# Where the weights and the moving operands of TensorE's products lie in the state buffer, modulo 256 bytes

## The chip, the core and the metric

The kernel runs on one core of a Trainium2 chip. The metric is the device time of one execution in microseconds (us). Before the change it is 2124.55 us, the median of three runs (2123.25 to 2124.76).

## The reference

One decoder layer for 512 tokens of width 2048, in float32:

```python
mod = silu(c) @ w_ada + b_ada                    # 6 x 2048: shifts, scales, gates
h   = rms_norm(x, g1) * (1 + sc1) + sh1
u   = h @ w_in                                   # split into conv and attention groups
y   = [rms_norm(short_conv(u)) | rms_norm(nsa_attention(u))]
x   = x + gate1 * (y @ w_out)
h   = rms_norm(x, g2) * (1 + sc2) + sh2
x   = x + gate2 * (relu(h @ w_ff1)**2 @ w_ff2)   # hidden width 8192
out = rms_norm(x, gf)
```

The attention has 8 heads in 2 groups with three branches (compressed keys, selected blocks, a window). What matters here are the large products: the projections from `h`, the two halves of the output projection, and the two feed-forward products.

## The kernel before

**Every large product is three.** A float32 operand is kept as a high part (rounded to the type float32r) and a low part (the rest). The function `mm3` issues high weights by high tokens, high weights by low tokens, and low weights by high tokens. The stationary operand of a TensorE instruction (the weights, 128 x 128 numbers, 512 bytes in each partition) is loaded by its own instruction ahead of the product; the moving operand has 512 columns (2048 bytes in each partition) or 256 (1024 bytes). ScalarE makes the high part and VectorE the low part of each weight tile after its DMA has landed (`weights` in the first stages, `hilo` in the last).

**Three stages**, each recorded into an `Order` and laid out by its planner. The planner gives each instruction a price (`price`; for TensorE 0.0015 us plus 0.000453 us a column), simulates engines, DMA and buffers in a list schedule, and emits the instructions in the order of the simulated beginnings. Products marked `floating` are placed wherever the plan has their inputs ready; others keep the order of their lanes.

1. *Projections and convolution* (to about 555 us): 512-column products. Weights come through `raw` (three tiles of the pool `stage`) into `wh` and `wl` (two each). The tokens are 16 tiles `h`: seven of them in the pool `side` (in the trace `h`), nine in main slots (`h_m`).
2. *Attention and the first half of the output projection* (to about 750 us): scores on `kslc` and `kwin`, transposes, `pv` products on `tt`, and 512-column products `pw` on `mix`, which lies in main slots.
3. *The rest*, from about 750 us. First the products on `mixa`: eight weight blobs with 512 columns (two still from `stage`, six through `hl_tile()`), then `late_out(0)` and `late_out(1)`, 256 columns each on eight kept blobs: three in `hl` tiles, one in `sg`, one in `gt`, three in main slots (`kw`). Each half ends in a norm (`half_norm`), whose few fp32 products with `ones` float into the stream of the others. Then the feed-forward.

**The feed-forward** uses a scheme of seven products for a 2 x 2 block product, with 256 columns each. `part` runs the first three blocks of hidden units (24 parts), `ff1(p)` the other 29; each `ff1(p)` makes seven weight operands and issues 7 x 24 products. Results go to DRAM by the GpSimd queue (`outcome`, from `gt` and `gb`), and come back as tokens `tk` for the second half, which for every f and q again makes seven operands with 4 + 4 times 12 products (7 x 24). `plain(3)` at the end does the last columns without the scheme.

**Addresses.** All tokens `tk`, `h_m`, `mix`, `mixa` lie in main slots of 4096 bytes, the first at byte 34304 of the partition, so all at multiples of 256. The tiles `h` lie 128 past a multiple of 256, `wh` and `wl` too; `tt` at 128, `vcmp` and `kslc` at 32, the feed-forward's `sg` and `gt` at 0. Within a tile the blocks of weights are 512 bytes and the blocks of tokens 1024 or 2048 bytes apart, so a whole tile has one difference. So the difference of the weights' address minus the moving operand's, modulo 256, is 128 for 512-column products on `h_m` and `mix`, and 0 for those on `h`.

The operands `wh, wl` of the feed-forward come from a ring of three `hl` tiles of 8640 bytes, in turn at bytes 203264, 220544 and 211904, and start at a shifting place in them:

```python
def hl_tile():
    j, t = next(hl)
    lo = (16 * shift[0] - j * HLW) % (16 * NSHIFT)
    return t[:, lo:lo + 1024], t[:, lo + 1024:lo + 2048]
```

`shift[0]` is p mod 8 in the first half and (4f + q) mod 8 in the second. With shift s the three turns of the ring start at 64s, 64s + 192 and 64s + 64 bytes modulo 256. So successive operands of one pass cycle through three of the four differences 0, 64, 128 and 192, and with s through all. One operand is 24 products in a row.

Of the kernel before, what the change touches and what calls it, by code (L numbers as in the profile page):

```python
# [9 lines left out]
F32 = mybir.dt.float32  # L10
F32R = mybir.dt.float32r
# [5 lines left out]
P = 128  # L17
# [11 lines left out]
BLOB = 1072  # L29
# [2 lines left out]
NSIDE = 7  # L32
NWA = 8
NBANK = 6
NSHIFT = 8
SLACK = 4.0
FAST = 395e3

# [2 lines left out]
C_COS, C_SIN, C_MASK, C_CMASK, C_ROW, C_END = 0, 512, 1024, 1152, 1280, 1281  # L41
# [3 lines left out]
class Order:  # L45
# [46 lines left out]
    def price(self, eng, op, out, ins, kw):  # L92

        n = Order.width(out)
        if "dma" in op:
            return (0.42 if eng == "sync" else 0.55), 0.0
        if eng == "tensor":
            if op == "matmul" and ins[0].dtype == F32:
                return max(0.25, n * 0.00182), 0.2
            return (0.109 if op == "transpose" else max(0.06, 0.0015 + n * 0.000453)), 0.2  # L100
        if eng == "scalar":
            aps = len(ins) - 1
            more = 0.1 if kw.get("accum_out") is not None else 0.0
            return (0.18 if n < 16 else 0.09 + 0.00084 * n + (0.09 * max(0, aps) if not more else 0.19)), 0.16
        if n < 16:
            return 0.1, 0.14
        if op == "scalar_tensor_tensor":
            return 0.14 + 0.00101 * n, 0.14
        if op in ("tensor_scalar", "tensor_copy", "memset"):
            return 0.13 + 0.0005 * n, 0.14  # L110
        if op == "tensor_reduce":
            n = max(Order.width(x) for x in ins) * (1.7 if n > 16 else 1)
        return 0.068 + 0.00104 * n, 0.14
# [177 lines left out]
def hybrid_layer(ctx: ExitStack, tc: tile.TileContext, a, out):  # L291
# [8 lines left out]
    attc = front.enter_context(tc.tile_pool(name="attc", bufs=1))  # L300
    stage = front.enter_context(tc.tile_pool(name="stage", bufs=2))
# [10 lines left out]
    ts = [small.tile([P, T], F32, name="t", tag="t", bufs=5) for _ in range(5)]  # L312
    scr, temps = ts[0].bitcast(BF16), cycle(ts[1:])
    accums = cycle([small.tile([P, T], F32, name="sacc", tag="acc2k", bufs=2) for _ in range(2)])
    wraw = cycle([stage.tile([P, BLOB], F32, name="raw", bufs=3) for _ in range(3)])
    whl = cycle([[stage.tile([P, BLOB + 16], F32R, name=n) for n in ("wh", "wl")] for _ in range(2)])
    accs = cycle([small.tile([P, 2], F32, name="acc") for _ in range(4)])

# [28 lines left out]
    def weights(src, cols=1024, spare=False):  # L347
        raw = next(wraw)[:, :cols]
        nc.sync.dma_start(out=raw, in_=src)
        wh, wl = (slot(F32R, name="sw") for _ in range(2)) if spare else next(whl)  # L350
        wh, wl = wh[:, :cols], wl[:, :cols]
        nc.scalar.activation(wh, raw, AF.Copy)
        nc.vector.tensor_tensor(out=wl, in0=raw, in1=wh.bitcast(F32), op=OP.subtract)
        return wh, wl
# [5 lines left out]
    def mm3(ps, lh, ll, rh, rl, start, stop, more=False):  # L360
        nc.tensor.matmul(ps, lh, rh, start=start, stop=False, skip_group_check=more)
        nc.tensor.matmul(ps, lh, rl, start=False, stop=False, skip_group_check=more)
        nc.tensor.matmul(ps, ll, rh, start=False, stop=stop, skip_group_check=more)
# [7 lines left out]
    ident = vec[:, V_ID:V_END]  # L371
    for i in range(NK // 2):
        nc.sync.dma_start(out=xs[i], in_=a["xt"][i])
    cst = attc.tile([P, C_END - C_MASK], F32, name="cst")
    cmask = cst[:, C_CMASK - C_MASK:C_ROW - C_MASK].rearrange("p (b n) -> p b n", b=NQ)
    rowv = cst[:, C_ROW - C_MASK:]
    mask = cst[:, :C_CMASK - C_MASK]
# [244 lines left out]
    for s, (name, k) in enumerate(steps[:-1]):  # L622
# [5 lines left out]
        wh, wl = w  # L628
# [96 lines left out]
    cw2 = pair(name="cw2").rearrange("p a b -> p (a b)")[:, :576]  # L725
    nc.sync.dma_start(out=cw2, in_=a["vec"][:, V_END:])

    edges = [[attc.tile([P, 66], F32R, name=f"edge{i}{j}") for j in range(2)] for i in range(2)]
    for e in edges:
        for x in e:  # L730
# [78 lines left out]
    for j in range(8):  # L809
# [4 lines left out]
        for i in range(3):  # L814
            n = 3 * j + i
# [30 lines left out]
    for g in range(NG):  # L846
        pv = [bank() for _ in range(NQ)]
        for blk in range(4):
            wh, wl = weights(a["w_v"][g * 4 + blk], BLOB)
            more_ada(1)  # L850
            for j in range(4):
                k = blk * 4 + j
# [45 lines left out]
    for g in range(NG):  # L898
        pq = [bank() for _ in range(NR)]
        ks = list(range(NK)) if g == 0 else list(range(8, NK)) + [6, 7] + list(range(6))  # L900
        for i, k in enumerate(ks):
            if i % 2 == 0:
                wh, wl = weights(a["w_q"][g * 8 + k // 2])
# [178 lines left out]
    while m < NK:  # L1082
        out_conv(m)
        m += 1
    oa = [weights(a["w_oa"][k]) for k in range(2)]
# [9 lines left out]
    ffp = ffn.enter_context(tc.tile_pool(name="ffp", bufs=2, reuse_waits="tile"))  # L1095
    psf = ffn.enter_context(tc.tile_pool(name="psf", bufs=8, space=PSUM, reuse_waits="tile"))
    HT = T // 2
    rw = cycle([ffp.tile([P, 1024], F32, name="rw", bufs=6) for _ in range(6)])
    gt = cycle([ffp.tile([P, 2, 2, HT], F32R, name="gt", bufs=3) for _ in range(3)])
    gb = cycle([ffp.tile([P, 2, HT], F32R, name="gb", bufs=1)])  # L1100
    p1s = cycle([ffp.tile([P, HT], F32, name="p1", bufs=3) for _ in range(3)])
    sg = {t: cycle([ffp.tile([P, 1024], d, name="sg", bufs=2) for _ in range(2)])
          for t, d in (("first", F32R), ("sums", F32), ("last", F32R))}
    HLW = 2048 + 16 * (NSHIFT - 1)
    hl = cycle([(j, ffp.tile([P, HLW], F32R, name="hl", bufs=3)) for j in range(3)])
    shift = [0]
    banks = cycle([psf.tile([P, T], F32, name="pf") for _ in range(8)])
    LO, HI = slice(0, HT), slice(HT, T)
    halves = (LO, HI)
# [2 lines left out]
    def bankf():  # L1112
        return next(banks)

    def raw_blob(src):
        raw = next(rw)
        nc.sync.dma_start(out=raw, in_=src)
        return raw

    def hl_tile():  # L1120
        j, t = next(hl)
        lo = (16 * shift[0] - j * HLW) % (16 * NSHIFT)
        return t[:, lo:lo + 1024], t[:, lo + 1024:lo + 2048]

    def hilo(dst, src, minus=False):
        if minus:
            nc.scalar.activation(dst[0], src, AF.Copy, scale=-1.0)
            nc.vector.scalar_tensor_tensor(out=dst[1], in0=src, scalar=-1.0, in1=dst[0].bitcast(F32),
                                           op0=OP.mult, op1=OP.subtract)
        else:  # L1130
            nc.scalar.activation(dst[0], src, AF.Copy)
            nc.vector.tensor_tensor(out=dst[1], in0=src, in1=dst[0].bitcast(F32), op=OP.subtract)
        return dst
# [18 lines left out]
    sacc = accum()  # L1152
    pm = [bankf() for _ in range(8)]
    for k in range(8):
        wh, wl = oa[k] if k < 2 else hilo(hl_tile(), raw_blob(a["w_oa"][k]))
        for i in range(8):
            s = slice(i * P, (i + 1) * P)
            mm3(pm[i], wh[:, s], wl[:, s], mixa[k][:, 0], mixa[k][:, 1], k == 0, k == 7)
# [41 lines left out]
    def tslot():  # L1200
        return slot(F32R, name="tk")[:, :4 * HT].rearrange("p (k h t) -> p k h t", k=2, h=2)
# [5 lines left out]
    def sub(dst, x, y, op=OP.subtract):  # L1207
        nc.vector.tensor_tensor(out=dst, in0=x, in1=y, op=op)
# [187 lines left out]
        if n in (17, 19, 23):  # L1396
            results_of({17: 2, 19: 0, 23: 1}[n])
    for p in range(NP, 32):
        shift[0] = p % NSHIFT
        ff1(p)  # L1400


# [84 lines left out]
    for f in range(8):  # L1487
        for i in range(7):
            for j in range(2):
                tok[i][j] = tslot()  # L1490
                nc.sync.dma_start(out=tok[i][j].bitcast(F32), in_=gd[f][i][j].bitcast(F32))
            if f == 0 and i == T5:
                residual_pairs()
        last = f == 7
        for q in range(3 if last else 4):
            shift[0] = (4 * f + q) % NSHIFT
            raw = [raw_blob(a["w_f2"][4 * f + q, b]) for b in range(4)]
            ps = [{}, {}]
            for i, w in enumerate(operands(raw)):
                if f == 0 and q < 3 and i == B2:  # L1500
                    residual_pairs()
                ch, first, end = CHAIN[i]
                for j in range(2):
                    mp = 2 * q + j
                    m = 2 * mp
                    if first:
                        ps[j][ch] = bankf()
                    run(ps[j][ch], w, tok[i], first, True, 4 * j, 4)
                    b = ps[j][ch][:, :HT]
                    if i == B1:  # L1510
                        if f == 0:
                            nc.scalar.activation(base[mp], b, AF.Copy)
                        else:
                            sub(base[mp], b, base[mp], OP.add)
                        if last:
                            shared(mp)
                    elif i == U6:
                        update(m, HI, b, True)
                    elif i == T5:
                        update(m + 1, HI, b, True)  # L1520
                    elif i == B2:
                        update(m, LO, b)
                        if last:
                            final(m, LO)
                    elif i == T7:
                        update(m + 1, HI, b)
                        if last:
                            final(m + 1, HI)
                    elif i == B3:
                        update(m, HI, b)  # L1530
                        if last:
                            final(m, HI)
                    else:
                        update(m + 1, LO, b)
                        if last:
                            final(m + 1, LO)
# [92 lines left out]
```

## Time and profile before

| | |
|---|---|
| median of 3 runs | 2124.55 us (2123.25 to 2124.76) |
| the profiled execution | 2124.95 us |
| its span, first to last instruction | 2123.2 us |
| TensorE products, weight loads | 14978, 14978 |
| mean granted TensorE clock | 0.994 of full speed |

Nearly all instructions pass through one helper, so the profile gives them one line (L121), and groups are told apart by their tiles: `pf<-tk,hl` is a product into a feed-forward bank with tokens `tk` and weights `hl`. The profile's mean time of one product (280 ns for 256 columns) is that from its start to its modelled end; products overlap, so the time that one costs in a stream is the distance from its start to the next one's start. A row of the timeline is a run of like instructions: start of the first, us to the end of the last, count. A row of the table by windows gives the busy time of each engine in a stretch, with the count of instructions that fall into it wholly or partly.

### The profile page before, as it was taken

How to read it: one execution, taken by the hardware profiler on the slowest of the kernel's cores; microseconds unless marked ns; L12 is line 12 of the kernel's file. 1: busy time of each engine (PE TensorE's matmuls, PEld its weight loads, DVE VectorE, ACT ScalarE, POOL GpSimd, SP SyncE). 2: the span in 40 equal slices, each digit the busy share in tenths (PEclk: the TensorE clock that was granted, in tenths of full speed). 3: DMA queues.
4: the chain of work that ended last, by engine and by line, in shares of the span. 5: the costliest groups of instructions: out<-in, count | busy, mean ns of one | idle time of the engine just before them, and what ended most of it. 6: DMA issues, size and time to landing. Idle time of an engine off the chain costs nothing.

```text
span 2123.2 us, 37933 instructions
## 1 busy us (share of the span) xinstructions
PE 2088.0 (98%) x14978; PEld 1941.9 (91%) x14978; DVE 1897.1 (89%) x3036; ACT 1006.0 (47%) x1472; POOL 128.2 (6%) x244
## 2 busy tenths in 40 slices
PE   7999999999999999999999999999999999999998
PEld 5888878898777789999999999999999999999997
DVE  8989988888998657999999999999998999999998
ACT  4432433222555435766666566666433333333345
POOL 0000000000000001021111211111000000000000
PEclk8999999999999999999999999999999999999999
DMA  8895689888421244476666666668876466366452
GB/s 341 338 351 217 219 295 323 303 290 290 148 80 40 70 168 159 145 220 217 194 199 204 204 199 198 214 193 302 307 265 218 139 248 236 126 244 236 134 188 90
DMA packets 143106, 454.17 MB, mean 214 GB/s; under 512 B 15824, under 2 KB 18128, under 8 KB 142928
## 3 DMA queue, kind: packets, MB, share of 16 engines
q1 hardware_dynamic: 108304, 386.72, 52.0%
q0 software_dynamic: 34048, 63.98, 9.6%
q8 instruction: 118, 1.93, 0.4%
q10 hardware_dynamic: 576, 1.05, 0.1%
q14 instruction: 60, 0.49, 0.1%
HBM read 383.53 MB, written 68.16 MB: 213 GB/s over the span
## 4 chain that ended last, share of the span: by engine, by line
PE 87%; DVE 9%; DMA 2%; issue 1%; ACT 1%; SPq 0%; DVEq 0%; ACTq 0%
PE pf L121 61%; PE ps L121 21%; PE pw L121 2%; DVE t L121 1%; PE pv L121 1%; DVE wl L121 1%; DVE nm L121 1%; DMA rw<-in_w_f 1%; DVE x L121 1%; DMA wa<-in_w_ada 1%; PE pt L121 1%; DVE tt L121 1%; DVE hl L121 1%; PE s L121 1%; DVE p L121 1%
## 5 line engine op out<-in xcount | busy, mean ns | idle before, releaser
L121 PE MATMUL pf<-tk,hl 128*128 128x256 f32 x10704 | 1251.4, 280 | 1.0 <-DVE x L121 0.5
L121 PEld LDWEIGHTS pf<-tk,hl 128*128 128x128 f32 x10704 | 1250.0, 189 | 1.4 <-issue 0.7
L121 ACT ACTIVATE hl<-rw 128x1024 fp32r<-128x1024 f32 x269 | 285.0, 1060 | 345.4 <-PE pf L121 291.2
L121 DVE TENSOR_TENSOR hl<-rw,hl 128x1024 fp32r<-128x1024 f32 x269 | 328.7, 1222 | 44.3 <-ACT hl L121 43.9
L121 ACT ACTIVATE hl<-sg 128x1024 fp32r<-128x1024 f32 x180 | 191.0, 1062 | 243.0 <-PE pf L121 222.1
L121 DVE SCALAR_TENSOR_TENSOR t<-wa,cs 128x1024 bf16<-128x1024 f32 x190 | 232.0, 1221 | 9.7 <-DMA wa<-in_w_ada 8.3
L121 PE MATMUL ps<-h_m,wh 128*128 128x512 f32 x720 | 227.7, 395 | 0.9 <-DVE h_m L121 0.9
L121 ACT ACTIVATE wh<-raw 128x1024 fp32r<-128x1024 f32 (+1 forms) x106 | 112.6, 1062 | 236.9 <-PE ps L121 200.8
L121 DVE TENSOR_TENSOR hl<-sg,hl 128x1024 fp32r<-128x1024 f32 x151 | 184.6, 1222 | 31.7 <-ACT hl L121 30.9
L121 PE MATMUL ps<-h,wh 128*128 128x512 f32 x560 | 172.7, 395 | 4.3 <-ACT h L121 4.3
L121 PEld LDWEIGHTS ps<-h_m,wh 128*128 128x128 f32 x720 | 134.9, 188 | 32.7 <-DVE h_m L121 1.2
L121 DVE TENSOR_TENSOR wl<-raw,wh 128x1024 fp32r<-128x1024 f32 (+1 forms) x106 | 129.9, 1226 | 30.1 <-ACT wh L121 29.7
L121 DVE SCALAR_TENSOR_TENSOR x<-pf,mod,x 128x256 f32<-128x256 f32 (+1 forms) x280 | 132.6, 488 | 17.1 <-PE pf L121 15.4
L121 DVE TENSOR_TENSOR sg<-sg,rw 128x1024 f32<-128x1024 f32 x120 | 146.2, 1219 | 0.0
L121 PE MATMUL ps<-h_m,wl 128*128 128x512 f32 x360 | 142.5, 396 | 0.0
L121 PEld LDWEIGHTS ps<-h,wh 128*128 128x128 f32 x560 | 105.6, 190 | 28.7 <-ACT h L121 6.7
L121 POOL DMA_DIRECT2D g<-gt x192 | 101.2, 532 | 373.1 <-issue 190.5
L121 PE MATMUL ps<-h,wl 128*128 128x512 f32 x280 | 106.2, 392 | 0.0
L121 PE MATMUL pw<-mix,wh 128*128 128x512 f32 x256 | 87.6, 404 | 0.0
L121 PEld LDWEIGHTS ps<-h_m,wl 128*128 128x128 f32 x360 | 67.7, 188 | 15.8
L121 DVE TENSOR_TENSOR sg<-rw 128x1024 f32<-128x1024 f32 x60 | 73.2, 1220 | 9.9 <-DMA rw<-in_w_f 6.8
L121 ACT ACTIVATE t<-t 128x512 f32<-128x512 f32 (+3 forms) x131 | 74.2, 571 | 15.9 <-DVE t L121 13.9
(225 smaller groups left out, 2151.1 us busy)
## 6 DMA issues: line engine op xcount, KB each, us to landing
rw<-in_w_f SPq DMA_DIRECT2D x263, 512.0 KB, 3.7
wa<-in_w_ada SPq DMA_DIRECT2D x192, 512.0 KB, 6.0
tk<-g SPq DMA_DIRECT2D x114, 512.0 KB, 6.3
g<-gt POOLq DMA_DIRECT2D x192, 256.0 KB, 3.4
raw<-in_w_conv SPq DMA_DIRECT2D x32, 512.0 KB, 4.7
x<-in_xt SPq DMA_DIRECT2D x16, 512.0 KB, 6.3
raw<-in_w_kv SPq DMA_DIRECT2D x16, 512.0 KB, 4.9
raw<-in_w_cv SPq DMA_DIRECT2D x16, 512.0 KB, 4.3
```

The costliest lines, as they stand in the source:

```text
L121: x.i, x.eng, x.call = len(self.nodes), eng, (lambda: real(*args, **kw))
```

## The change

It alters addresses and one price; no instruction is added or removed.

- `hl_tile(lo=0)` no longer shifts: both halves start at a fixed place, and the tiles are 8448 bytes (33 x 256). A tile `skip` of 192 bytes ahead of `gt`, which nothing uses, moves all behind it in that pool: `gt`, `gb`, `p1`, `sg` and `hl` start 192 past a multiple of 256. All weight operands of the feed-forward in `hl`, `sg` and `gt` then lie at difference 192. The blobs for the 512-column products on `mixa` are placed 64 bytes further (`hl_tile(16)`), at difference 0. The three late output blobs in main slots stay at 0.
- In the first two stages `cst` grows to 1280 bytes, a tile `fill` of 224 bytes is added ahead of `edges`, and `raw` grows to 4352 bytes. By the widths of the tiles ahead of them, `kslc`, `vcmp`, `raw`, `wh`, `wl`, `h` and `tt` then start at multiples of 256, and the 512-column products on `h`, `h_m`, `mix` and `tt` all have difference 0 (the second rows of `kslc` lie 128 further by their width).
- The planner's price of a TensorE product falls to 0.0015 us plus 0.000441 us a column, so all three orders are planned anew.

```diff
-NSHIFT = 8
...
-            return (0.109 if op == "transpose" else max(0.06, 0.0015 + n * 0.000453)), 0.2
+            return (0.109 if op == "transpose" else max(0.06, 0.0015 + n * 0.000441)), 0.2
...
-    wraw = cycle([stage.tile([P, BLOB], F32, name="raw", bufs=3) for _ in range(3)])
+    wraw = cycle([stage.tile([P, BLOB + 16], F32, name="raw", bufs=3) for _ in range(3)])
...
-    cst = attc.tile([P, C_END - C_MASK], F32, name="cst")
+    cst = attc.tile([P, 320], F32, name="cst")[:, :C_END - C_MASK]
...
+    attc.tile([P, 56], F32, name="fill")
     edges = [[attc.tile([P, 66], F32R, name=f"edge{i}{j}") for j in range(2)] for i in range(2)]
...
     rw = cycle([ffp.tile([P, 1024], F32, name="rw", bufs=6) for _ in range(6)])
+    ffp.tile([P, 48], F32, name="skip", bufs=1)
     gt = cycle([ffp.tile([P, 2, 2, HT], F32R, name="gt", bufs=3) for _ in range(3)])
...
-    HLW = 2048 + 16 * (NSHIFT - 1)
-    hl = cycle([(j, ffp.tile([P, HLW], F32R, name="hl", bufs=3)) for j in range(3)])
-    shift = [0]
+    hl = cycle([ffp.tile([P, 2112], F32R, name="hl", bufs=3) for _ in range(3)])
...
-    def hl_tile():
-        j, t = next(hl)
-        lo = (16 * shift[0] - j * HLW) % (16 * NSHIFT)
+    def hl_tile(lo=0):
+        t = next(hl)
         return t[:, lo:lo + 1024], t[:, lo + 1024:lo + 2048]
...
-        wh, wl = oa[k] if k < 2 else hilo(hl_tile(), raw_blob(a["w_oa"][k]))
+        wh, wl = oa[k] if k < 2 else hilo(hl_tile(16), raw_blob(a["w_oa"][k]))
...
     for p in range(NP, 32):
-        shift[0] = p % NSHIFT
         ff1(p)
...
         for q in range(3 if last else 4):
-            shift[0] = (4 * f + q) % NSHIFT
             raw = [raw_blob(a["w_f2"][4 * f + q, b]) for b in range(4)]
```

## The prediction

> **What bounds the kernel now.** I read the page first (busy shares, then the chain of waits), then a table by stage.
>
> ```profile
> PE 2088.0 (98%) x14978; PEld 1941.9 (91%) x14978; DVE 1897.1 (89%) x3036; ACT 1006.0 (47%) x1472; POOL 128.2 (6%) x244
> PE 87%; DVE 9%; DMA 2%; issue 1%; ACT 1%; SPq 0%; DVEq 0%; ACTq 0%
> ```
>
> ```profile
> core 0: us, PE busy (x) PEld busy (x) DVE busy (x) ACT busy (x) POOL busy (x), PEclk, DMA share, GB/s
> 850.00:1480.00 630.00, 630.00 (x5401) 630.00 (x5400) 580.95 (x804) 401.37 (x577) 115.06 (x218) 1.00 0.66 206
> 1560.00:2040.00 480.00, 480.00 (x4116) 480.00 (x4115) 448.42 (x620) 181.91 (x172) 0.00 (x0) 1.00 0.58 203
> 550.00:735.00 185.00, 179.02 (x917) 138.93 (x915) 158.77 (x432) 94.78 (x249) 0.00 (x0) 1.00 0.19 63
> 1480.00:1560.00 80.00, 79.00 (x675) 78.63 (x674) 73.78 (x101) 34.90 (x43) 5.26 (x10) 1.00 0.92 327
> 2040.00:2124.00 84.00, 72.88 (x615) 72.10 (x614) 73.72 (x135) 44.82 (x87) 0.00 (x0) 0.95 0.28 95
> ```
>
> The chain is 87% matmul. In the feed-forward stages (850 to 1480, 1560 to 2040) TensorE has no idle time and the full clock, so their length is the number of products times the distance from one start to the next. A window also counts products already under way at its edge, 280 ns long each (row below), 2.4 of them: 630.00/(5401-2.4) = 116.7 ns, 480.00/(4116-2.4) = 116.7 ns. VectorE is busy 92% and 93% there, close behind. The change alters nothing but addresses, so what matters is how that distance depends on them, and the kernel before shows it: its 256-column products stand at all four differences.
>
> ```profile
> L121 PE MATMUL pf<-tk,hl 128*128 128x256 f32 x10704 | 1251.4, 280 | 1.0 <-DVE x L121 0.5 <-DVE hl L121 0.5
> 1181.12 5.68 PE L121 MATMUL pf<-tk,hl 128*128 128x256 f32 x46
> 1298.71 5.61 PE L121 MATMUL pf<-tk,hl 128*128 128x256 f32 x46
> 1102.54 5.49 PE L121 MATMUL pf<-tk,hl 128*128 128x256 f32 x47
> 985.29 5.38 PE L121 MATMUL pf<-tk,hl 128*128 128x256 f32 x46
> 1122.35 5.58 PE L121 MATMUL pf<-tk,hl 128*128 128x256 f32 x46
> 1128.01 2.75 PE L121 MATMUL pf<-tk,hl 128*128 128x256 f32 x22
> ```
>
> These timeline rows run from the first start to the last end, so the distance is (length - 0.28)/(x - 1). The difference (weights minus moving operand, mod 256) follows from the placement told above. Difference 0: 5.40/45 = 120.0 ns. 128: 118.4. 64: 113.3. 192: 113.3. But the fifth row is also 64 and gives 5.30/45 = 117.8, and the sixth is 192 and gives 2.47/21 = 117.6. So **64 and 192 have two beats**, one of 113.3 ns and one of 117.8 ns. The 1128.01 block follows directly on the 1122.35 block: the beat is carried from product to product.
>
> **The change part by part.** *The new address difference, in the feed-forward.* 10704 products of `pf<-tk,hl`, 96 with `sg` and 48 with `gt` weights: 10848 at difference 192 instead of a mixture at 116.7 ns. Which beat they take decides everything: 10848 x (113.3-116.7) = -36.9 us, or 10848 x (117.8-116.7) = +11.9 us. To choose, I looked at how each beat is entered.
>
> ```profile
> 859.25 2.66 PE L121 MATMUL pf<-tk,hl 128*128 128x256 f32 x22
> 2042.59 2.77 PE L121 MATMUL pf<-tk,hl 128*128 128x256 f32 x23
> ...
> 821.33 0.59 PE L121 MATMUL pf<-t,ones 128*128 128x256 f32 x2
> 822.00 1.70 PE L121 MATMUL pf<-mixa,hl 128*128 128x256 f32 x13
> ...
> 845.20 0.61 PE L121 MATMUL pf<-ones,sacc 128*128 128x1 f32 x4
> 847.18 0.59 PE L121 MATMUL pf<-t,ones 128*128 128x256 f32 x2
> 847.42 0.59 PE L121 MATMUL pf<-tk,sg 128*128 128x256 f32 x2
> 848.44 2.16 PE L121 MATMUL pf<-tk,hl 128*128 128x256 f32 x17
> ...
> 2102.39 0.59 PE L121 MATMUL pf<-t,ones 128*128 128x256 f32 x2
> 2103.05 0.87 PE L121 MATMUL pf<-tk,hl 128*128 128x256 f32 x6
> ```
>
> The first two rows are blocks at 192 that come straight after a block at 0: 113.3 and 113.2 ns, an early one and a late one of the 73 such successions in the trace, which are all fast. The others are the three places where the norm's fp32 products (`ones`) interrupt the stream and products at 192 come next: 1.42/12 = 118.3, 1.88/16 = 117.5 and 0.59/5 = 118.0 ns, all slow. After the change the last 256-column products at difference 0 are the late output products whose weights lie in main slots; behind them comes the second norm half (845.20 and 847.18 in the rows) among products at 192, and from there to the end every 256-column product is at 192. The one way into the fast beat that the trace shows, a block at 0, is gone, and the norm's interruption leads into the slow one. Inside the blocks no change of beat shows at an unchanged difference, and TensorE runs without a gap for 600 us. So I take the slow beat: +11.9 us, less 0.4 for the blocks around the stalls, **+11.5**. The other bound is -36.9.
>
> *The 512-column products* go from 128 (`h_m`, `mix`, first `mixa` blocks) to 0, where those on `h` already stand.
>
> ```profile
> 94.70:116.40 21.70, 21.70 (x97) 1.00 0.98 360
> 485.20:532.70 47.50, 47.50 (x205) 1.00 0.81 292
> ...
> L121 PE MATMUL ps<-h_m,wh 128*128 128x512 f32 x720 | 227.7, 395 | 0.9 <-DVE h_m L121 0.9
> L121 PE MATMUL ps<-h_m,wl 128*128 128x512 f32 x360 | 142.5, 396 | 0.0
> L121 PE MATMUL pw<-mix,wh 128*128 128x512 f32 x256 | 87.6, 404 | 0.0
> L121 PE MATMUL pw<-mix,wl 128*128 128x512 f32 x128 | 52.2, 408 | 0.0
> ```
>
> By the same reckoning (395 ns long, so 1.7 extra in a window) the first window, `h` at 0, gives 21.70/95.3 = 227.8 ns, the second, `h_m` at 128, 47.50/203.3 = 233.6: 5.8 ns apart. 1080 products on `h_m` save 6.3 us, 384 on `mix` 2.2. The latter lie in attention (550 to 735), where TensorE idles 6 us for others and VectorE is busy 86%, so I count half of them: 6.3+1.1 = 7.4, and of that **-7.0**, since the projections begin behind VectorE. Bounds: -9 if all of it holds (the smaller `mixa` and `pv` groups too), -2.5 if what waits on VectorE and ScalarE takes the rest back.
>
> *The late output products* (256 columns on `hl`, `sg`, `gt`): 144 of them were at 0, about 3 to 7 ns each: -0.5 us.
>
> *Moved tiles.* `gt` now starts 192 past a multiple of 256, and it is a source of DMAs:
>
> ```profile
> g<-gt POOLq DMA_DIRECT2D x192, 256.0 KB, 3.4
> ```
>
> Three tiles serve one pass of 168 products, 168 x 116.7 ns = 19.6 us; even a doubled landing (6.8 us) is covered by that, so 0. Uncovered it would be three tiles x 3.4 us a pass at worst. The raw, `fill` and `skip` tiles add no instruction: 0.
>
> *The planner's price* for a TensorE product falls by 2.6%, so all three plans are made anew. Nothing is added; a different order can cost or gain at the waits, which are these in the feed-forward:
>
> ```profile
> 1526.57 8.33 PE L121 MATMUL pf<-tk,hl 128*128 128x256 f32 x70 [0.48 <-DVE hl L121]
> 1535.42 9.83 PE L121 MATMUL pf<-tk,hl 128*128 128x256 f32 x81 [0.52 <-DVE x L121]
> ```
>
> About 1 us there (a slower TensorE gives VectorE that much back: -0.7). I take 0 for the order itself, bounds -3 to +3, half the 6 us of attention's idle time.
>
> *Sum:* 11.5-7.0-0.5-0.7 = +3.3 on a span of 2123.2: 2126.5. The profiled execution took 2124.95, 1.75 more than its span and 0.4 above the median shown (2124.55). So 2126.5+1.75-0.4 = 2127.9, **2128**.
>
> A rule that speaks against any effect: the Trainium skill, "TensorE: Matmul & The Clock Gate", section "Step-by-step: what each phase is for", says that TensorE reads the moving operand and the weights through two independent ports, so that loading the next weights takes nothing from the running product. By that rule the difference of addresses would be worth 0 and the time 2124.5; the rows above, 120.0 against 113.3 ns for one shape at one clock, disagree.
>
> **The rivals.** *R1, the fast beat holds throughout.* For it: 113.3 is much the commoner beat at 192, and nothing in the trace shows what a long run at one difference does. Against: the entries above. Time: -36.9-7.4-0.5 = -44.8, so 2079.8; VectorE would then be busy 580.95/630 x 116.7/113.3 = 95% and in the second stage 96%, so a few waits are likely: 2081.
>
> *R2, one half of the feed-forward fast, the other slow.* At 1520 to 1535 TensorE stops twice and starts again; that may throw the beat either way. With the second half (some 4900 products) fast and the first (5900) slow: +6.5-16.7-8 = -18, 2106. The other way round, -20+5.4-8 = -23: 2101.
>
> *R3, slower.* The slow beat in the feed-forward as forecast, and attention and the projections give no time back, because each matmul that ends earlier there only waits longer for the operand that VectorE makes (its wait stands at the head of these stages). The price is the 512-column saving: 11.5-0.5-1 = +10, 2134. It decides from the point where the first 750 us shorten by less than 3 us. Against: 408 products run without a gap from 116.5 to 211.6, a VectorE that is not late there.
>
> *R4, the difference does nothing:* 2124.5. The four rows per difference speak against it.
>
> **How the numbers follow.** Forecast (slow beat, 512-column saving kept) 0.37, its own range 2123 to 2132; R1 0.25; R2 0.23; R3 0.11; R4 0.02; the rest scattered by the new order. A measurement of this kernel can tell about 0.2% from no change, 4.25 us: faster is below 2120.3, slower above 2128.8. R1, R2 and a little of the forecast (a lucky order) make faster 0.53; some six tenths of the forecast, R4 and scattered ones make same 0.26; the forecast's upper end and R3 make slower 0.21. The range runs from R1 without new waits, 2078, to short of R3, 2132; some 0.05 lies below and 0.1 above.
>
> **What would show it.** In the stage 850 to 1480 the distance of `pf<-tk,hl` products: 117.8 ns if I am right, 113.3 under R1, a change of beat at a stop under R2. `h_m` products at 227 to 228 ns and the first feed-forward product about 7 us earlier if the second step is right; the same start as before under R3. If 113.3 ns follows directly on the norm's `ones` products, my reading of the entries is wrong, and with it the forecast.

## The result and the profile after

| | before | after |
|---|---|---|
| median | 2124.62 us (2123.25 to 2124.76) | 2140.85 us (2140.46 to 2141.01) |
| span of the profiled execution | 2123.2 us | 2138.7 us |
| mean granted TensorE clock | 0.994 | 0.989 |

The changed kernel is slower: its time is 1.0078 of the one before, with an interval of 1.0060 to 1.0095. That is 12.85 us above the forecast of 2128 and above the end of the range, 2132.

The page of the changed kernel: its busy shares, the clock in 40 slices and two groups of products.

```profile
PE 2095.9 (98%) x14978; PEld 1958.7 (92%) x14978; DVE 1906.9 (89%) x3036; ACT 1005.7 (47%) x1472; POOL 128.2 (6%) x244
PEclk8999999999899999999999999999999999999999
L120 PE MATMUL pf<-tk,hl 128*128 128x256 f32 x10704 | 1262.9, 279 | 0.0
L120 PE MATMUL ps<-h_m,wh 128*128 128x512 f32 x720 | 224.1, 390 | 0.9 <-DVE h_m L120 0.9
```

The number of products is the same and TensorE is busy 7.9 us longer. One digit of the clock row, the eleventh slice (535 to 588 us), has fallen to 8. The 512-column products on `h_m` are shorter, 224.1 us busy for 227.7.

The table by windows of the changed kernel, first the two feed-forward stages, then three places around attention:

```profile
core 0: us, PE busy (x) PEld busy (x) DVE busy (x) ACT busy (x) POOL busy (x), PEclk, DMA share, GB/s
850.00:1480.00 630.00, 630.00 (x5351) 629.95 (x5350) 578.43 (x799) 397.95 (x574) 113.97 (x216) 1.00 0.66 200
1560.00:2040.00 480.00, 480.00 (x4078) 480.00 (x4078) 448.11 (x612) 180.33 (x170) 2.11 (x4) 1.00 0.57 204
551.50:565.20 13.70, 10.11 (x29) 7.94 (x29) 11.07 (x33) 3.07 (x12) 0.00 (x0) 0.50 0.31 115
740.90:748.60 7.70, 7.70 (x34) 6.18 (x33) 6.46 (x10) 5.93 (x10) 0.00 (x0) 1.00 0.10 39
752.90:759.70 6.80, 4.85 (x11) 3.80 (x12) 5.31 (x6) 0.00 (x0) 0.00 (x0) 0.50 0.56 199
```

By the reckoning of the prediction the distance between feed-forward products is 630.00/(5351-2.4) = 117.8 ns, and 480.00/(4078-2.4) = 117.8: the slow beat everywhere. In the row from 551.50 and in the last TensorE has half its clock, for 13.7 and 6.8 us; each row spans just the stretch with that clock. Outside of the start and the end of the span the kernel before has no such stretch.

Rows of the timeline of the changed kernel: start, length to the last end, count, and in brackets how long TensorE stood idle and what ended it.

```profile
549.52 1.23 PE L120 MATMUL s<-kslc,q 128*128 128x160 f32 x9 [2.87 <-ACT qr L120]
553.38 0.80 PE L120 MATMUL pw<-mix,wl 128*128 128x512 f32 x1 [2.11 <-DVE wl L120]
558.44 0.93 PE L120 MATMUL s<-kslc,q 128*128 128x160 f32 x3 [1.71 <-DVE pc L120]
754.85 0.80 PE L120 MATMUL pf<-mixa,wl 128*128 128x512 f32 x1 [5.63 <-DVE wl L120]
846.69 2.88 PE L120 MATMUL pf<-tk,hl 128*128 128x256 f32 x24
```

The same places in the timeline of the kernel before:

```profile
556.23 1.24 PE L121 MATMUL s<-kslc,q 128*128 128x160 f32 x9 [1.44 <-ACT qr L121]
560.14 0.57 PE L121 MATMUL s<-kslc,q 128*128 128x160 f32 x3 [0.54 <-DVE pc L121]
750.65 0.50 PE L121 MATMUL pf<-mixa,wl 128*128 128x512 f32 x1 [0.59 <-DVE wl L121]
841.01 3.04 PE L121 MATMUL pf<-tk,hl 128*128 128x256 f32 x24
```

Two starts cut the span into three parts: the first score (`s<-kslc`) and the first feed-forward product (`pf<-tk,hl`). The projections, with the wait at their end, became 6.7 us shorter (556.23 to 549.52). Attention and the output products became 12.4 us longer (841.01-556.23 = 284.78 to 846.69-549.52 = 297.17). The feed-forward became 9.8 us longer (2123.2-841.01 = 1282.2 to 2138.7-846.69 = 1292.0). The sum is the +15.5 of the spans. The first and the third part go nearly as forecast; the second was forecast at no loss.

The waits for `qr` and `pc` are larger, the one of 2.11 us for `wl` at 553 us is new, and the one at 750 us has grown from 0.59 to 5.63 us. What leads up to the last is seen in one row of the table by windows of the kernel before, against the row from 740.90 above:

```profile
735.60:749.40 13.80, 13.80 (x60) 11.07 (x59) 12.61 (x20) 7.33 (x11) 0.00 (x0) 1.00 0.15 59
```

Both rows begin behind the `ones` products of attention's norm, on whose result VectorE makes the tiles for the products on `mixa`, and end about where the first of those starts. They show the products that TensorE has left meanwhile, `pw` nearly all of them. Before there were 60 of them (13.8 us), now 34 (7.7 us): the new order spends them earlier, and TensorE runs dry 6 us sooner.

### The profile page after: what moved, and what is told of

Its sections match the earlier page's. It is cut to its first block, busy times and chain, and to the rows that moved or that the text cites. A ratio compares the mean times of both kernels' runs of the same rounds, so it can differ in the third digit from the quotient of the medians.

```text
span 2138.7 us, 37934 instructions
## 1 busy us (share of the span) xinstructions
PE 2095.9 (98%) x14978; PEld 1958.7 (92%) x14978; DVE 1906.9 (89%) x3036; ACT 1005.7 (47%) x1472; POOL 128.2 (6%) x244
## 4 chain that ended last, share of the span: by engine, by line
PE 90%; DVE 7%; issue 1%; ACT 0%; DMA 0%; SPq 0%; DVEq 0%; ACTq 0%
PE pf L120 64%; PE ps L120 21%; PE pw L120 2%; DVE t L120 2%; PE pv L120 1%; DVE wl L120 1%; PE s L120 1%; PE pt L120 1%; DVE nm L120 1%; DVE tt L120 1%; DVE p L120 0%; DMA wa<-in_w_ada 0%; DVE x L120 0%; DVE s L120 0%; DVE ya L120 0%
## 5 line engine op out<-in xcount | busy, mean ns | idle before, releaser
L120 ACT ACTIVATE wh<-raw 128x1024 fp32r<-128x1024 f32 (+1 forms) x106 | 112.8, 1064 | 266.9 <-PE ps L120 227.8
L120 PE MATMUL ps<-h_m,wh 128*128 128x512 f32 x720 | 224.1, 390 | 0.9 <-DVE h_m L120 0.9
L120 PE MATMUL pw<-mix,wh 128*128 128x512 f32 x256 | 92.4, 415 | 0.0
L120 PEld LDWEIGHTS ps<-h_m,wl 128*128 128x128 f32 x360 | 67.6, 188 | 13.8
```

What stands on the lines that cost most here:

```text
L120: x.i, x.eng, x.call = len(self.nodes), eng, (lambda: real(*args, **kw))
```

## The experiments

For the loss beyond the forecast, theory O says that it is the new order alone, made by the planner's price; the rival says that the addresses themselves cost it. For the feed-forward, theory H says that the beat is held from product to product and a block at difference 0 sets it; its rival L says that a block at 0 makes fast only what follows it closely. The medians of the kernel before beside these runs were 2125.1, 2124.7 and 2125.2 us.

**1. The new addresses with the old price.**

```diff
-max(0.06, 0.0015 + n * 0.000441)
+max(0.06, 0.0015 + n * 0.000453)
```

> The changed kernel's addresses with the planner's old price (0.000453 us a column). Two questions. The wait of 5.6 us at 748.6 us: if the new price made it (theory O, order), it is gone here, attention is ordered as in the kernel before, and the time is 2128 to 2133 us; if the faster 512-column products made it (theory A, addresses), it stays, and the time is within 3 us of 2141. The beat: both theory H (history: the beat at difference 192 is set by what came before and then kept) and theory L (length: a long stretch at 192 always ends in the slow beat) expect 117.8 ns in the feed-forward.

Measured: 2130.6 us (2128.69 to 2132.46), 1.0026 of before (1.0016 to 1.0037). 10.3 of the 16.2 us are gone. The timeline of this run, whose span is 2128.2 us:

```profile
550.79 1.23 PE L120 MATMUL s<-kslc,q 128*128 128x160 f32 x9 [1.44 <-ACT qr L120]
745.79 0.50 PE L120 MATMUL pf<-mixa,wl 128*128 128x512 f32 x1 [0.87 <-DVE wl L120]
835.45 2.88 PE L120 MATMUL pf<-tk,hl 128*128 128x256 f32 x24
```

The waits for `qr` and ahead of the products on `mixa` are small again, and the clock is full there. By parts: projections -5.4, attention and output products 284.66 (-0.1), feed-forward 2128.2-835.45 = 1292.75 (+10.6). Theory O is right. The traces say it directly, too: by the names of their tiles, TensorE's products stand in one and the same order in this run and in the kernel before, and in another in the changed kernel.

**2. The old addresses with the new price**, in the kernel before.

```diff
-max(0.06, 0.0015 + n * 0.000453)
+max(0.06, 0.0015 + n * 0.000441)
```

> The kernel before with the new price alone (0.000441 us a column), old addresses. Theory O: a wait of several us ahead of the mixa products also here, 2129 to 2135 us. Theory A: no such wait, 2122 to 2128 us. The feed-forward stays at 116.7 ns by all.

Measured: 2137.06 us (2134.65 to 2137.35), 1.0053 of before (1.0038 to 1.0068), 2 us above what theory O gave. Its timeline:

```profile
557.02 1.23 PE L121 MATMUL s<-kslc,q 128*128 128x160 f32 x9 [2.86 <-ACT qr L121]
762.22 0.80 PE L121 MATMUL pf<-mixa,wl 128*128 128x512 f32 x1 [5.48 <-DVE wl L121]
854.67 3.04 PE L121 MATMUL pf<-tk,hl 128*128 128x256 f32 x24
```

The span is 2135.6 us. Without any new address the same two waits stand there, and attention with the output products takes 854.67-557.02 = 297.65 us, 12.9 more than before. The price alone costs it, whatever the addresses; the order of the products is that of the changed kernel.

**3. Only the 512-column products** (`cst`, `fill` and `raw` as in the change, the rest as before, old price).

```diff
-    wraw = cycle([stage.tile([P, BLOB], F32, name="raw", bufs=3) for _ in range(3)])
+    wraw = cycle([stage.tile([P, BLOB + 16], F32, name="raw", bufs=3) for _ in range(3)])
...
-    cst = attc.tile([P, C_END - C_MASK], F32, name="cst")
+    cst = attc.tile([P, 320], F32, name="cst")[:, :C_END - C_MASK]
...
+    attc.tile([P, 56], F32, name="fill")
```

> The kernel before with the address changes of the first two stages alone (cst, fill, raw), old price, old feed-forward. If the 512-column saving reaches the end: 2116 to 2120 us, first feed-forward products 5 to 8 us earlier, 227 ns on h_m. If waits on VectorE and ScalarE give it back (the rival R3 of the prediction): 2123 to 2126 us with 227 ns on h_m all the same.

Measured: 2121.76 us (2120.56 to 2124.39), 0.9986 of before (0.9976 to 0.9996): -3.3 us, between the two expectations. The products themselves have the forecast distance (table by windows of this run; the kernel before has 409 products in the first of these windows):

```profile
116.50:211.60 95.10, 95.10 (x422) 78.75 (x421) 88.39 (x148) 28.17 (x32) 0.00 (x0) 1.00 0.76 281
0.00:553.70 553.70, 532.18 (x2572) 442.26 (x2572) 491.92 (x839) 196.69 (x257) 0.20 (x4) 0.98 0.81 295
```

95.10/(422-1.7) = 226.3 ns against 95.10/(409-1.7) = 233.5. The second row goes to the first score; the row of the kernel before that answers to it:

```profile
0.00:556.20 556.20, 537.52 (x2572) 443.22 (x2572) 492.70 (x839) 196.69 (x257) 0.20 (x4) 0.98 0.80 294
```

TensorE is busy 5.3 us less, and the first score comes only 2.5 us earlier. One wait of TensorE in that part, in this run and then in the kernel before (us in total, times, longest):

```profile
PE ps L121 <- ACT sw L121: 3.7, 4, 1.5
```

```profile
PE ps L121 <- ACT sw L121: 0.8, 1, 0.8
```

2.9 us went into waits for `sw` tiles, which ScalarE makes. So half of the saving was taken back there, in this execution. In the run of the first experiment, with the same addresses, price and order in this stage, the first score is 5.4 us earlier than before, so what is taken back differs between executions. Behind the first score, whose wait is 1.44 us as before, TensorE had half its clock here for 3.4 us, which the kernel before and the first experiment do not show:

```profile
555.60:559.00 3.40, 3.26 (x10) 2.15 (x9) 3.08 (x14) 0.53 (x3) 0.00 (x0) 0.50 0.86 247
```

**4. One block at difference 0 ahead of the long stream.** To the first experiment: the first weight operand of `ff1(3)`, at 905 us, lies 64 bytes further, so its 24 products are at 0.

```diff
-    def operands(raw, minus=False):
+    def operands(raw, minus=False, lo=0):
...
-        yield hilo(hl_tile(), a11)
+        yield hilo(hl_tile(lo), a11)
...
-        for i, w in enumerate(operands(raw, True)):
+        for i, w in enumerate(operands(raw, True, 16 if p == NP else 0)):
```

> As e1, but the first weight operand of the first ff1 pass lies 64 bytes further, at difference 0: one block of 24 products at 0 in some 10,800 at 192. Theory H: from that block on 113.3 ns, at least until the stop at about 1520 us; 2108 us when the slow beat comes back there, 2083 to 2086 us when the fast one lasts to the end. Theory L: the fast beat is lost again within a few blocks, time within 2 us of e1.

Measured: 2109.79 us (2108.47 to 2110.55), 0.9927 of before (0.9912 to 0.9942), 20.8 us less than the first experiment. Table by windows of this run:

```profile
910.00:1478.00 568.00, 568.00 (x5014) 568.00 (x5014) 533.46 (x718) 360.51 (x502) 107.62 (x204) 1.00 0.71 222
1481.00:1505.00 24.00, 24.00 (x206) 24.00 (x205) 21.74 (x30) 10.27 (x13) 2.63 (x5) 1.00 0.96 326
1560.00:2040.00 480.00, 480.00 (x4078) 480.00 (x4077) 447.72 (x620) 185.75 (x184) 0.00 (x0) 1.00 0.54 194
```

568.00/(5014-2.4) = 113.3 ns for more than 5000 products behind 24 products at 0. At 1479.5 us two starts lie 0.32 us apart; behind them 24.00/(206-2.4) = 117.9 ns, and 117.8 to the end of the second half. Theory L has fallen, and H holds in the main. A block at 0 does not lead into the fast beat everywhere, though: the 24 products right behind the 72 with `kw` weights at 0 have 117.8 ns in this run (2.99 us from 836.33, so 2.71/23), as in the fifth and the eleventh; in the changed kernel and five other runs they have 113.3. Behind the blocks of 24 that were put at 0 for these experiments, 69 in the six runs that have them, the beat is fast each time.

**5. The same at the first pass of each f of the second half**, added to the fourth.

```diff
-            for i, w in enumerate(operands(raw)):
+            for i, w in enumerate(operands(raw, lo=16 if q == 0 else 0)):
```

> As e4, with a second kind of reset: in each f of the second feed-forward product the first weight operand of the first pass also lies at difference 0 (eight more blocks of 24 at 0). Theory H: in the second half the fast beat comes back at the first f after the stops at 1480 to 1515 us, and the time is about 21 us below e4, 2087 to 2092 us; with VectorE 96% busy there a stop may end it again within an f, then up to 2100 us. Theory L: as e4, 2108 to 2111 us.

Measured: 2093.93 us (2091.88 to 2095.54), 0.9853 of before (0.9838 to 0.9867). This version beats both kernels, the one before by 31 us. Table by windows of this run:

```profile
1560.00:2040.00 480.00, 480.00 (x4229) 480.00 (x4228) 459.19 (x642) 193.45 (x193) 0.00 (x0) 1.00 0.56 198
```

480.00/(4229-2.4) = 113.6 ns, the blocks at 0 included. VectorE is busy 96% of that stage (459.19 of 480), as R1 had it, and TensorE still never waits there.

**6. A block at 0 in every pass of the second half**, and one in the last of the first 24 parts.

```diff
-            dst = hl_tile()
+            dst = hl_tile(16 if n == 5 else 0)
...
-            for i, w in enumerate(operands(raw)):
+            for i, w in enumerate(operands(raw, lo=16)):
```

> As e5, with the reset in every pass of the second half (31 blocks of 24 at 0) and in part 5 of the first blocks. Theory H: if the fast beat holds within an f anyway, the 23 more blocks at 0 cost 23 x 24 x 6.7 ns = 3.7 us and the earlier reset gives back about 2 us: 2 us above e5. If it is lost within an f, it is up to 10 us below e5.

Measured: two executions at 2093.92 and 2095.87, eight at 2112.47 to 2116.74, median 2114.57. The expectation fails for most executions. Table by windows and timeline of one of the slower ones:

```profile
860.00:910.00 50.00, 50.00 (x442) 50.00 (x441) 46.21 (x80) 34.59 (x59) 7.41 (x14) 1.00 0.62 197
920.00:1470.00 550.00, 550.00 (x4673) 550.00 (x4672) 502.93 (x674) 342.24 (x476) 105.32 (x200) 1.00 0.66 205
```

```profile
908.08 5.49 PE L120 MATMUL pf<-tk,hl 128*128 128x256 f32 x47
914.04 2.63 PE L120 MATMUL pf<-tk,hl 128*128 128x256 f32 x21
917.30 7.89 PE L120 MATMUL pf<-tk,hl 128*128 128x256 f32 x65 [0.63 <-DVE t L120]
```

It is fast up to 910 us (113.7 ns, the fourth experiment's block at 905 included) and behind that block (5.21/46 = 113.3 in the first row). At 913.8 us two starts lie 0.29 us apart, with no idle time that the timeline shows, and from the second row on the beat is slow: 2.35/20 = 117.5 ns, and 550.00/4670.6 = 117.8 in the rest of `ff1`. The stop of 0.63 us ahead of 917.30 finds the slow beat already there. Nothing resets it until the second half, which is fast. That the two executions at 2094 and 2096 us kept the fast beat in `ff1` fits their time, 20 us less; no trace of them was taken, so it is not shown.

**7. The feed-forward at difference 64 in place of 192** (to the first experiment; the other beat pair of the kernel before).

```diff
-    ffp.tile([P, 48], F32, name="skip", bufs=1)
+    ffp.tile([P, 16], F32, name="skip", bufs=1)
...
-hilo(hl_tile(16), raw_blob(a["w_oa"][k]))
+hilo(hl_tile(48), raw_blob(a["w_oa"][k]))
```

> As e1 with the feed-forward's weights at difference 64 in place of 192. Difference 64 has the same two beats in the kernel before, but there a block at 0 leads into its slow beat. Theory H: the beat after the norm's fp32 products is kept; slow (117.8 ns) gives e1's time, 2129 to 2132 us; fast (113.3 ns) some 2082 us; which of the two no trace so far shows. Theory L for both differences: 2129 to 2132 us.

Measured: five executions at 2108 to 2116 and five at 2129 to 2133, median 2122.61, 0.9987 of before (0.9958 to 1.0016). The profiled one, 2131 us, is slow in the first stage:

```profile
850.00:1480.00 630.00, 630.00 (x5351) 630.00 (x5350) 577.01 (x796) 396.05 (x567) 115.07 (x218) 1.00 0.66 205
```

No verdict on 64 against 192 comes out of it. The profiled execution is at 117.8 ns there; that the faster five were at 113.3 in one of the halves fits their time, 20 us less, and is not shown.

**8. One fp32 product of one column ahead of the eighth pass of `ff1`**, added to the fourth; its result is unused.

```diff
+        if p == 10:
+            nc.tensor.matmul(bankf()[:, 0:1], ident, ones[:, 0:1], start=True, stop=True)
```

> As e4, with one fp32 product of one column (on ident and ones, its result unused) put into TensorE's stream ahead of the eighth ff1 pass, in the fast stretch at about 1040 us. Theory H with interruptions as the cause of the slow beat: 117.8 ns from there to the stop at 1480 us, some 23 passes x 168 x 4.4 ns = 17 us above e4, 2124 to 2128 us. If only a stop of TensorE, not another kind of product, ends the fast beat: within 1.5 us of e4.

Measured: 2110.63 us (2108.95 to 2114.39), 0.8 above the fourth: no change of beat. Table by windows of this run, before and behind the product at 1040.7:

```profile
920.00:1035.00 115.00, 115.00 (x1017) 115.00 (x1016) 108.82 (x147) 73.56 (x102) 23.33 (x45) 1.00 0.69 209
1045.00:1470.00 425.00, 425.00 (x3752) 425.00 (x3751) 399.65 (x539) 271.63 (x380) 81.25 (x154) 1.00 0.71 221
```

113.3 ns on both sides. This fp32 product does not end the fast beat. At 1482.0 us, where two starts lie 0.20 us apart with no idle time shown, the slow beat begins in this run too.

**9. Blocks at 0 in every fourth pass of `ff1` and every second pass of the second half.**

```diff
+        for i, w in enumerate(operands(raw, True, 16 if p % 4 == NP else 0)):
...
+            for i, w in enumerate(operands(raw, lo=16 if q % 2 == 0 else 0)):
```

> As e1 with a block at difference 0 at the head of every fourth ff1 pass (8) and of every second pass of the second half (16). Theory H: each reset brings the fast beat back after whatever stop ended it, so the time is within 4 us of e5 (2090 to 2098 us) and the executions agree better than those of e6. Theory that the stops of a fast TensorE (VectorE late) eat the gain: above 2100 us.

Measured: 2097.82 us (2095.2 to 2099.72), 0.9865 of before (0.9851 to 0.988), 3.9 above the fifth and within the expected range. More blocks at 0 gain nothing more where the beat holds anyway.

**10. The change, with the old price in attention's plan only.**

```diff
+    pe = 0.000441
...
-max(0.06, 0.0015 + n * 0.000441)
+max(0.06, 0.0015 + n * self.pe)
...
+    order.pe = 0.000453      # the Order of attention
```

> The changed kernel with the old price in the planner of the attention stage alone; the projections and the feed-forward keep the new one. If the attention's order made the wait of 5.6 us at 748.6 us and the half clock behind it: that wait under 1.5 us, about 8 us off, 2130 to 2135 us; the wait of 2.9 us at 549.5 us stays. If it follows from the projections' order: 2138 to 2142 us. Feed-forward at 117.8 ns in both.

Measured: 2136.06 us (2134.82 to 2136.8), 1.0045 of before (1.003 to 1.006): 4.8 us of the 10.3 are attention's plan, less than expected. Timeline and table by windows of this run, whose span is 2134.0 us:

```profile
551.50 2.21 PE L121 MATMUL s<-kslc,q 128*128 128x160 f32 x9 [2.87 <-ACT qr L121]
752.03 0.50 PE L121 MATMUL pf<-mixa,wl 128*128 128x512 f32 x1 [0.92 <-DVE wl L121]
841.63 2.88 PE L121 MATMUL pf<-tk,hl 128*128 128x256 f32 x24
```

```profile
550.70:564.40 13.70, 10.46 (x32) 8.13 (x33) 13.06 (x35) 3.32 (x13) 0.00 (x0) 0.50 0.51 167
```

The wait at 752 us is small again, and between the `ones` products of attention's norm and the first product on `mixa` TensorE again has 13.6 us of products (736.95 to 750.50), so it belongs to attention's plan. The wait of 2.87 us for `qr` and the 13.7 us at half clock behind it remain. Attention and output products take 841.63-551.50 = 290.13 us, 5.5 more than in the first experiment. TensorE's products in attention stand in the order of the first experiment here, those of the other stages in the order of the changed kernel. The 5.5 us lie between the first score and the first `wl` product on `mixa` (752.03-551.50 = 200.53, there 745.79-550.79 = 195.00); from there to the feed-forward it is 89.6 against 89.7, and the feed-forward (2134.0-841.63 = 1292.4) is as long as there. So this remainder comes from the plan of the projections, under which TensorE waits 2.87 us for `qr` in place of 1.44, and not from that of the last stage.

**11. One fp32 product of 256 columns, of the norm's kind, at the place of the eighth experiment.**

```diff
+        if p == 10:
+            nc.tensor.matmul(bankf()[:, :HT], ones, r2[:, LO], start=True, stop=True)
```

> As e8 (itself e4 and one more product), but the added fp32 product has 256 columns, as the norm's spread has, ahead of the eighth ff1 pass at about 1040 us. If this kind of product leads into the slow beat, as it did at 821, 847 and 2102 us in the kernel before: 117.8 ns from there to 1480 us, 2124 to 2128 us. If it does not: within 2 us of e4, and the norm's slow beat comes from its stops or its order.

Measured: 2126.63 us (2124.24 to 2131.05), 16.8 above the fourth, as expected. Timeline and table by windows of this run:

```profile
1039.62 0.59 PE L120 MATMUL pf<-sacc,ones 128*128 128x256 f32 x2
```

```profile
920.00:1035.00 115.00, 115.00 (x1017) 115.00 (x1017) 108.50 (x147) 74.28 (x103) 22.84 (x44) 1.00 0.70 210
1045.00:1470.00 425.00, 425.00 (x3611) 425.00 (x3610) 388.07 (x519) 262.24 (x366) 80.76 (x154) 1.00 0.67 207
```

113.3 ns before it (115.00/1014.6), 117.8 ns behind it (425.00/3608.6), with no idle time between. This single product (the profile counts it as two) throws the beat, as the norm's products do. Whether it does so by its kind or only by the time it takes (the first two products behind it start 0.31 us apart, those behind the one of the eighth experiment 0.20) is open.

## Why the prediction was wrong

The span, by the same two starts. "Price" says which price made the plans.

| part, us | forecast | after | 1: new addresses, old price | 2: old addresses, new price | 3: 512 columns only | 10: old price in attention |
|---|---|---|---|---|---|---|
| projections | about -6 | -6.7 | -5.4 | +0.8 | -2.5 | -4.7 |
| attention, output products | about -1.5 | +12.4 | -0.1 | +12.9 | +0.5 | +5.3 |
| feed-forward | +10.8 | +9.8 | +10.6 | -1.3 | +0.1 | +10.2 |
| span | +3.3 | +15.5 | +5.0 | +12.4 | -1.9 | +10.8 |

(The forecast of the feed-forward is +11.5 for the beat less 0.7 at the stalls.)

**The step that failed is the planner's price**: "I take 0 for the order itself, bounds -3 to +3". The medians give 2140.85-2130.6 = +10.3. The bound was half the idle time that attention had, and that is no bound: a new order can make new idle time. It made two places of it. The projections' plan leaves `qr` late (2.87 us for 1.44), and attention's plan uses up the `pw` products that cover VectorE's work for `mixa` (60 down to 34), so that the wait there goes from 0.59 to 5.63 us. Both cost more than the wait, for TensorE then has half its clock for 13.7 and 6.8 us. In the 14 us from 550 the new order gets 34 products done and the first experiment 66:

```profile
550.00:564.00 14.00, 10.17 (x34) 7.76 (x34) 12.57 (x36) 3.07 (x12) 0.00 (x0) 0.56 0.39 145
```

```profile
550.00:564.00 14.00, 11.69 (x66) 9.61 (x67) 13.62 (x45) 6.21 (x22) 0.00 (x0) 1.00 0.33 113
```

(The first fence is the changed kernel, the second the first experiment. The two orders differ, so the counts are of products of unequal size; with one order of products, the tenth experiment against the first, the stretch at half clock and the waits in it cost 5.5 us.) The first experiment is 2.6 us above the forecast, so this step is 10.3 of the 12.85 us missed. The prediction named the bound by idle time without asking what a stall does to the clock. Why a price 2.6% lower gives these orders was not tried; that it alone does so is shown by the second experiment, whose products stand in the order of the changed kernel.

A rule that bears on this stands in the Trainium skill, "TensorE: Matmul & The Clock Gate", section "What's actually happening": the clock halves after an idle window of about 3.4 us, and a busy one gives it back. The stretches agree, for 6.8 and 13.7 us are two and four times 3.4. The stretch of 6.8 us begins 3.7 us after TensorE fell idle at 749.2, as the rule has it. That a window of full idleness is needed does not agree: the longest single stop ahead of the 13.7 us is 2.87 us (they begin 2 us behind its end in the changed kernel, and within it in the tenth experiment), and in the third experiment 3.4 us of half clock follow a stop of 1.44 us.

**The beat was right.** The slow beat was chosen over the fast one, and 117.8 ns stands in both stages. The entry that it rested on, the norm, was right too: in the changed kernel the products behind the last block at 0 are fast, and behind the norm's `ones` products they are slow. The other one, a block at 0, was read as surer than it is: behind the `kw` blocks three of the nine runs at difference 192 are slow. Timeline of the changed kernel:

```profile
844.77 2.08 PE L120 MATMUL pf<-mixa,kw 128*128 128x256 f32 x16
846.69 2.88 PE L120 MATMUL pf<-tk,hl 128*128 128x256 f32 x24
849.41 2.88 PE L120 MATMUL pf<-tk,sg 128*128 128x256 f32 x24
...
854.01 0.59 PE L120 MATMUL pf<-t,ones 128*128 128x256 f32 x2
...
855.86 2.99 PE L120 MATMUL pf<-tk,gt 128*128 128x256 f32 x24
```

2.60/23 = 113.0 ns in the two rows behind `kw`, 2.71/23 = 117.8 in the last. The term of +11.5 less the stalls measured +10.6 (first experiment) and +9.8. That nothing later would bring the fast beat back was partly luck: the changed kernel has no stop near 1530 us any more, and in the sixth experiment one there did bring it back. That the beat is carried on was read from blocks of 24 products; the fourth experiment shows it over 5000. R1 and R2 fall for this kernel, and the fourth and fifth experiments are their cases made on purpose: 2109.79 for the first half fast (R2 had 2101), 2093.93 for nearly all of it (R1 had 2081).

**The 512-column term was mis-sized**: -7.0 forecast, -3.3 by the median of the third experiment, near the bound of -2.5; the first experiment, with the same addresses, gained 5.6 us in the first two parts in its profiled execution. The distance was right (226.3 ns measured, forecast 227.8). What was wrong was to count the time of the products as time of the stage: in the third experiment, of 5.3 us that TensorE had less to do in the projections, 2.9 went to waits for `sw`. That is R3's mechanism, at a smaller size and within the projections. R3's condition, that the first 750 us shorten by less than 3 us, is met in one of the two and not in the other: the first feed-forward product comes 2.0 us earlier than before in the third experiment (839.00) and 5.6 in the first. Its time of 2134 is not reached without the new order: the first experiment took 2130.6.

**The rest held.** The moved tiles cost nothing that shows: with the old price the feed-forward is as long as the beat alone makes it, and `g<-gt` lands in 3.3 us there, 3.4 before. R4, no effect of the addresses, has fallen by the fourth experiment, where 64 bytes under 24 products are worth 20.8 us.

**What stays open**: why the difference of addresses sets the distance at all, and what decides the beat where the stream is broken. It goes either way: two starts 0.40 us apart at 1480.0 in the fifth experiment left the fast beat standing, and 0.62 us at 1536.1 in the sixth brought it back. Once it changed with neither a stop nor another product (in the fifth, from 113 to 118 ns at 2054.3 us).

## What to carry to other kernels

A price in a planner is a change of its own, whatever stands beside it in the diff: it must be costed by the work that covers each wait in the new order, and not by the idle time of the old one. A stall of some 3 us on TensorE cost twice here, once as idle time and once as half clock behind it. Where TensorE sets the end, look at the distance between products block by block, against the addresses of both operands: here a fixed difference with nine blocks at difference 0 (the fifth experiment) is worth 1.5% against the kernel before.

## What the runs showed of the hardware

- Products of one shape, one address difference (192) and one clock run at 113.3 or 117.8 ns, and keep what they have over as long as 568 us. The fast beat followed all 69 blocks of 24 products put at difference 0, but the 72 `kw` products at 0 in only six of the nine runs at that difference.
- A single fp32 product of 256 columns is followed by the slow beat without idle time (113.3 to 117.8 ns); one of a single column is not (113.3 on both sides).
- A delay between two starts can be followed by the slow beat (0.20 us in place of 0.113 at 1482 us in the eighth experiment, 0.29 at 914 in the sixth, 0.32 at 1479 in the fourth) or not (0.40 at 1480 in the fifth). The same kernel can come out 20 us apart between executions (2094 and 2115 us; 2108 and 2133 us); that the beat makes this difference is likely, not shown.
- Half clock came with waits of 2.87 us (13.7 us long) and of 5.63 us (6.8 us long). Where no wait at the first scores was longer than 1.74 us, five of ten runs show 3.4 us of it (third, fourth, fifth, sixth, eighth) and five none.
